# Latent attention: a second set of keys for odd heads, and another order of its pieces

## The chip, the cores and the metric

The kernel runs on one core of a Trainium2 chip. Its time is the device time of one launch in microseconds (us). A core has TensorE (PE; PEld is its weight load), VectorE (DVE), ScalarE (ACT), GpSimd (POOL) and the queue engine SyncE (SP), each of which runs its own instructions in order and waits for the others by semaphores.

## The reference, cut to what matters

One step of a two-layer backbone on 512 latent and 128 prompt tokens. Layer 0 has eight latent-attention (MLA) heads beside eight neighbourhood heads; layer 1 has grouped-query attention; a SwiGLU block follows each. The change lies in the latent heads of layer 0:

```python
def mla_expand(ckv, w_ukv, k_rope):
    kv = (ckv @ w_ukv).reshape(b, L, MLA_HEADS, MLA_NOPE_DIM + MLA_V_DIM)
    k_nope, v = kv[..., :MLA_NOPE_DIM], kv[..., MLA_NOPE_DIM:]
    k_r = jnp.broadcast_to(k_rope[:, :, None, :], (b, L, MLA_HEADS, MLA_ROPE_DIM))
    return jnp.concatenate([k_nope, k_r], axis=-1), v
...
    a_mla = attend_blocked(q, jnp.concatenate([k_lat, k_ctx], axis=1),
                           jnp.concatenate([v_lat, v_ctx], axis=1), MLA_SCALE)
```

The 512 latent queries attend to 640 keys (512 latent and 128 cached), the 128 prompt queries only to the prompt's 128 keys.

## The kernel before, in words

All activations lie with features on partitions. A float32 operand x is split in a rounded high part h and a low part l = x - h, both in the fast matmul type; a product is then three matmuls (h h, h l, l h). So each operand made on the chip costs a copy on ScalarE (h) and a subtraction on VectorE (l).

**Keys.** A key has 64 own features and 64 rows of rotary features (kr, the same for all heads). Two heads share one product `mk` (`k_pieces`, L843): rows 0 to 63 are the even head's own features, rows 64 to 127 the odd head's. There is one tile set for even heads, `kT[.][0]` and one for odd heads, `kT[.][1]` (h and l, 640 columns of which the scores use all), and a small tile `kTp` with the prompt's keys of both. The rotary half of each is written once, in neighbourhood head 6 (L920); the other half is written again for every pair p, by `k_set` (L830) through two products: `k0` (512 latent keys) and `k1` (128 cached and 128 prompt keys).

**Pieces of a head.** Heads run in order 0 to 7. A head h has four score pieces `s0` to `s3` (128 queries by 640 keys: six matmuls `ms`, the negative maximum `mn` on VectorE, the exponential into `mp` on ScalarE, the reciprocal of the sum `mr` on VectorE, the scaling on POOL); then, one head later, `t0` to `t4` (four transposes each into `mt`, split into `mts_0` to `mts_4`) and `v0` to `v4` (matmuls with the values into one bank `mo`). `v3` and `v4` run one head later still, under the names `w3` and `w4`; after them the two halves of `mo` are added into `oM` by way of `mhs`. `sp` is the prompt's scores (`mpp0s` for pair 0), `pt` the transposes of a pair's two prompt weights and their split (`mpp0pth`, `mpp0ptl`), `pv` the product with the prompt's values (`mpp0o`), then added into `oM`. `q0` and `q1` make the next head's query (`mq`; `mqt` on VectorE, `mqh` on ScalarE, `mql` on POOL). `oNs` are splits of the neighbourhood heads' outputs, put in behind the last exponential of heads 0, 2, 4 and 5, and `oaw` weights of the following projection.

**Order.** The order of the pieces on TensorE is written by hand, in `MLA_ORDER` (L999), one string for even and one for odd heads, and in `NA_ORDER` (L880) for the neighbourhood heads, of which the last, head 7, makes the first pair's keys and query. Each piece is issued behind the last matmul of the piece ahead; the order on ScalarE, VectorE and POOL is set by a scheduler out of the dependencies.

In an odd head, `k0` and `k1` write the even set's rows at once. The odd set is still read by this very head's `s3` and `sp`, so its rows are written by separate pieces, `e0` behind `s3` and `e1` behind `sp`; until then the products' PSUM banks stay taken.

**PSUM.** The pool `m` has four banks, used in turn by all of `q`, `t`, `pt`, `pv`, `k`, `sp` and `mo`; `mo` is held from `v0` of a head to `w4` in the next. The scores have two double banks of their own (`bank2`), so `s2` waits until the exponential of `s0` is done.

Of the kernel before, what the change touches and what calls it, by code (L numbers as in the profile page):

```python
# [12 lines left out]
F32R = mybir.dt.float32r  # L13
# [38 lines left out]
def body(ctx, tc, xT, vecs, crow, wm0, wm0g1, wm0g, wm1, wA, wNV, wNA, wMK, wMV, wOA, wGQ, wGK, wGV, wOC,  # L52
# [130 lines left out]
    def mm3(ps, a, b, h, l, st, sp, **k):  # L183
        PE.matmul(ps, a, h, start=st, stop=False, **k)
        PE.matmul(ps, a, l, start=False, stop=False, **k)
        PE.matmul(ps, b, h, start=False, stop=sp, **k)
# [217 lines left out]
    def scores(pss, q, kh, kl):  # L404

        a, b = q
        for i, (c0, c1) in enumerate(HALF):
            PE.matmul(pss[:, i, :HT], a, kh[:, c0:c1], start=True, stop=False)
        for i, (c0, c1) in enumerate(HALF):
            PE.matmul(pss[:, i, :HT], a, kl[:, c0:c1], start=False, stop=False)  # L410
        for i, (c0, c1) in enumerate(HALF):
            PE.matmul(pss[:, i, :HT], b, kh[:, c0:c1], start=False, stop=True)
# [90 lines left out]
    hh, hl = hm.hh, hm.hl  # L503
    pss = [pair(f"wA{u}") for u in range(2)] + [[bank(f"wA2{c}") for c in range(2)]]
# [7 lines left out]
    with tc.tile_pool(name="start", bufs=1) as big:  # L512
# [9 lines left out]
        w3 = [unit(wA[0], 1024, "wA0")]  # L522
# [50 lines left out]
    kr = keep.tile([P, 768], F32, name="kr")  # L573
# [22 lines left out]
    for c, (c0, c1) in enumerate(HALF):  # L596
        ps = pss[2][c]
        V.tensor_tensor(ka[0:32, c0:c1], ps[0:32, :HT], tk[0:32, c0:c1], ALU.mult)
        done = V.tensor_tensor(kb[0:32, c0:c1], ps[32:64, :HT], tk[32:64, c0:c1], ALU.mult)
# [3 lines left out]
    pss = [pair(f"ckv{u}") for u in range(2)]  # L603
# [15 lines left out]
    for kk in range(4):  # L619
# [3 lines left out]
        for j in range(2):  # L623
            k = 2 * kk + j
            a, b = wh[:, 512 * j:512 * (j + 1)], wl[:, 512 * j:512 * (j + 1)]
            for i in range(5):
                c0, c1 = P * i, P * i + P
# [19 lines left out]
    for r in range(2):  # L647
        hr, lr = STACK[r]
        src = ckf[hr, :512].rearrange("p (a b) -> p a b", b=P)
# [177 lines left out]

    KPART = ((0, 512), (512, 640), (640, 768))

    def k_set(r, rows, parts, src):  # L830

        jobs = []
        for c in parts:
            c0, c1 = KPART[c]
            o = c0 - KPART[parts[0]][0]
            h, l = [(kTp[i][r] if c == 2 else kT[i][r][:, c0:c1])[rows] for i in range(2)]
            jobs.append((h, l, src[rows, o:o + c1 - c0]))
        for h, l, part in jobs:
            S.activation(h, part, AF.Copy)
        for h, l, part in jobs:  # L840
            V.tensor_tensor(l, part, f(h), ALU.subtract)

    def k_pieces(p, bk):  # L843

        out = {}
        for c, n in ((0, 512), (1, 256)):
            parts, box = ((0,), (1, 2))[c], []

            def done(ps, parts=parts, box=box):
                box.append(ps)  # L850
                k_set(0, slice(0, 64), parts, ps)

            def other(parts=parts, box=box):
                k_set(1, slice(64, 128), parts, box[0])
            (out[f"k{c}"],) = pieces_of(f"mk{p}{c}", bk, lambda: mla_w(p), *[t for t in lat[c]], [0, 1], 0, n, done)
            out[f"e{c}"] = other
        return out

    mqs, exps = {}, {}
# [14 lines left out]
    def ybank(name):  # L874
# [4 lines left out]
    tail, oN = {}, []  # L879
    NA_ORDER = ["s0 q0 t0 t1 q1 m0 q2 s1 v0 t2 sp q3 q4 v1 q5 m1 v2 q6 pt q7 m2 pv",  # L880
                "s0 q0 t0 t1 q1 m0 q2 s1 v0 t2 sp q3 q4 v1 q5 q6 q7 m1 v2 pt m2 pv"] * 3
    NA_ORDER += ["s0 t0 t1 pt m0 s1 v0 t2 sp m1 v1 pv v2 m2", "s0 t0 t1 k0 s1 e0 v0 t2 sp k1 v1 u0 e1 v2 u1"]
    M_AT = 1, 3, 5, 6
    for h in range(8):
        p, r = divmod(h, 2)
        if r == 0:
            oN.append(ring.tile([P, T], F32, tag="x", name=f"oN{p}"))
            pfirst, psecond = prompt_pair([nv[4][:, 2 * p + i, :] for i in range(2)], oN[p], ab, f"npp{p}",
                                         lambda name: bank(name, "y"))
        pts = []  # L890
        sc = na_scores(h, bm, pts)
        if h < 7:
            bm = na_bias(h + 1)
        qh, ql, ks = [t[r] for t in nqk[p]]
        pieces = named("s", sc)

        def prompt_scores(pss, qh=qh, ql=ql, ks=ks):
            PE.matmul(pss, qh[:, NS:T], ks[:, 896:1024], start=True, stop=False)
            PE.matmul(pss, ql[:, NS:T], ks[:, 896:1024], start=False, stop=True)
        pieces["sp"] = pfirst(r, prompt_scores)  # L900
        if p < 3:
            pieces.update(named("q", na_q(p + 1) if r == 0 else na_k(p + 1)))
        for n, at in enumerate(M_AT):
            if h == at:
                pieces.update(named("n" if "m0" in pieces else "m", mod0(4 + n, lambda n=n: bank(f"mod{4 + n}", "y"), mod_raw)))
        if h == 7:
            pieces.update(k_pieces(0, ybank))
            pieces.update(named("u", q_pieces(0, ybank, lambda c: ring.tile([P, T], F32R, tag="h" + c, name=f"mq{c}0"),
                                              lazy(lambda: load(tabM[:, 0, :], T, "tq0")))))
        sequence(NA_ORDER[h], {**pieces, **tail})  # L910
        tail = na_values(h, pts, oN[p])
        if r == 1:
            tail.update(psecond)
        if h == 6:
            cqs = [rsplit(cq[u], f"cqs{u}") for u in range(2)]
            lat = latents()
            kT = [[ring.tile([P, T], F32R, tag="h" + c, name=f"kT{c}{r}") for r in range(2)] for c in "hl"]
            kTp = ring.tile([P, T], F32R, tag="x", name="kTp")
            kTp = [[kTp[:, P * (2 * i + r):P * (2 * i + r + 1)] for r in range(2)] for i in range(2)]
            for r in range(2):  # L920
                k_set(r, (slice(64, 128), slice(0, 64))[r], (0, 1, 2), kr)
            mla_w(0)
            wmv = unit(wMV, 1024, "wmv")
# [17 lines left out]
    tq = cp.tile([P, 2, T], F32, name="tq")  # L941
    nc.sync.dma_start(tq, tabM)
    mv = [cp.tile([P, 8, P], F32R, name=f"mv{i}") for i in range(6)]
    for i, pss in mvb.items():
        vsplit(mv[i], pss)
    open_y(s=2)
# [4 lines left out]
    def mla_scores(h, pts):  # L951
        r = h % 2
        ll = tiny.tile([P, 4], F32, tag="ll", bufs=4, name=f"ml{h}")

        def piece(j):
            qh, ql = mqs[h]
            pss = bank2(f"ms{h}_{j}")
            scores(pss, (qh[:, P * j:P * j + P], ql[:, P * j:P * j + P]), kT[0][r], kT[1][r])
            nm = tiny.tile([P, 1], F32, tag="nm", name=f"mn{h}_{j}")
            V.tensor_reduce(nm, pss[:, :, :HT], AX.XY, ALU.max, negate=True)  # L960
            pt = cp.tile([P, T], F32, tag="mp", bufs=8, name=f"mp{h}_{j}")
            exps[h, j] = S.activation(halves(pt), pss[:, :, :HT], AF.Exp, bias=nm, accum_out=ll[:, j:j + 1])
            softmax_tail(pt, ll[:, j:j + 1], f"mr{h}_{j}", T)
            pts.append(pt)
        return [lambda j=j: piece(j) for j in range(4)]
# [28 lines left out]
    for i in range(6):  # L994
        if i not in mvb and i not in BESIDE:
            mv_late(i)
    tail, oM, oNs = {}, [], []

    MLA_ORDER = ("s0 w3 q0 w4 s1 t0 t1 pt s2 v0 t2 q1 v1 t3 s3 pv v2 t4 sp",  # L999
                 "s0 w3 q0 w4 s1 t0 t1 q1 s2 k0 v0 t2 s3 e0 v1 k1 t3 sp e1 t4 v2")  # L1000
    late = {}
    for h in range(8):
        p, r = divmod(h, 2)
        if r == 0:
            oM.append(cp.tile([P, T], F32, tag="om", bufs=4, name=f"oM{p}"))
            pfirst, psecond = prompt_pair([mv[5][:, 2 * p + i, :] for i in range(2)], oM[p], cp, f"mpp{p}",
                                         bank)
        pts = []
        sc = mla_scores(h, pts)
        qh, ql = mqs[h]  # L1010
        pieces = named("s", sc)
        pieces["sp"] = pfirst(r, lambda pss, qh=qh, ql=ql, r=r: mm3(pss, qh[:, NS:T], ql[:, NS:T], kTp[0][r], kTp[1][r], True, True))
        if h == 0:
            pieces.update({f"b{i}": lambda i=i: mv_late(i) for i in BESIDE})
        if h < 7:
            pieces.update(named("q", mla_q(h + 1)))
            if r == 1:
                pieces.update(k_pieces(p + 1, qbank))
        sequence(MLA_ORDER[r], {**pieces, **late, **{k: v for k, v in tail.items() if k not in ("v3", "v4")}})
        late = {"w" + k[1]: tail[k] for k in ("v3", "v4") if k in tail}  # L1020

        def out_m(ps, h=h, p=p, r=r):
            half_sum(((oM[p][64 * r:64 * r + 64, 0:NS], 0, NS),), ps, NS, cp, f"mhs{h}")
        tail = values(h, pts, lambda b, th, tl, h=h: [(mv[b][:, h, :], th), (mv[b][:, h, :], tl)], cp, "m", out_m)
        if r == 1:
            tail.update(psecond)
        if h in (0, 2, 4, 5):
            oNs.append(after(exps[h, 3], lambda: rsplit(oN[len(oNs)], f"oNs{len(oNs)}")))
# [654 lines left out]
    hh, hl = box2["m"].hh, box2["m"].hl  # L1683
# [374 lines left out]
```

## Time and profile before

| | us |
|---|---|
| median of 3 runs | 1501.86 (1498.52 to 1502.44) |
| profiled execution | 1503.23 |
| its span, first to last instruction | 1501.2 |
| busy TensorE / VectorE / ScalarE / POOL | 1448.7 / 1233.7 / 786.2 / 176.3 |
| the latent heads, first score matmul to the last head's | 223.76 to 321.17 |

One execution was profiled. "L64" in its rows is line 64 of the kernel, the helper through which all matmuls go; so a matmul is told by its tiles: `ms<-kTh,mqh` writes tile ms from kTh and mqh. A row of a timeline gives the start, the length, the engine, the line, the operation, output and inputs, and in brackets how long the engine stood idle ahead of it and who ended that. The timeline merges like neighbours (x4). "PEclk" is the share of full TensorE clock that was granted.

### The profile page before, as it was taken

To read this page: it belongs to the slowest core of one execution; us is meant where nothing else is said; L and a number is where in the kernel's file an instruction comes from. 1 tells how busy PE (TensorE), PEld (TensorE's weight loads), DVE (VectorE), ACT (ScalarE), POOL (GpSimd) and SP (SyncE) were. 2 spreads that over 40 slices of the span, in tenths; PEclk is the share of its full clock that TensorE was granted. 3 is DMA by queue.
4 is the path that set the end of the run, shared out by engine and by line. 5 is a ranking of instruction groups with operands and counts; after the bars stand their busy time and mean duration, and the time that the engine had idled before them with its cause. 6 is when DMAs were issued, how large, how long until landed. Compare 5 with 4: busy or idle time off the path is not lost. (4 is left out here: it accounts for less than half of the span.)

```text
span 1501.2 us, 25833 instructions
## 1 busy us (share of the span) xinstructions
PE 1448.7 (96%) x9766; PEld 1392.8 (93%) x9766; DVE 1233.7 (82%) x2375; ACT 786.2 (52%) x1539; POOL 176.3 (12%) x272
## 2 busy tenths in 40 slices
PE   5999989899999999999999999999999999999997
PEld 4989978889899999999999999989899999999996
DVE  5877778877788888955898887887899989889976
ACT  5446677763635555532122656673565555655443
POOL 0046636420000000000000122220100000000000
PEclk9999999999999999999999999999999999999999
DMA  9653341015055555549775311115245555548561
GB/s 375 202 152 121 114 145 43 15 64 204 29 207 164 170 171 168 162 169 341 231 229 169 103 33 36 37 41 185 68 157 169 193 170 191 175 154 297 181 263 71
DMA packets 79636, 231.48 MB, mean 154 GB/s; under 512 B 8856, under 2 KB 13240, under 8 KB 79128
## 3 DMA queue, kind: packets, MB, share of 16 engines
q1 hardware_dynamic: 77152, 225.43, 45.0%
q10 hardware_dynamic: 1944, 3.48, 0.7%
q8 instruction: 76, 1.25, 0.3%
q0 software_dynamic: 416, 0.93, 0.2%
q14 instruction: 48, 0.39, 0.1%
HBM read 193.15 MB, written 36.66 MB: 153 GB/s over the span
## 5 line engine op out<-in xcount | busy, mean ns | idle before, releaser
L1627 DVE SCALAR_TENSOR_TENSOR junk<-wm,cb 128x1024 bf16<-128x1024 f32 x88 | 107.2, 1218 | 3.4 <-DMA wm<-in_wm 2.8
L64 PE MATMUL gq<-h10h,wgq 128*128 128x320 f32 x256 | 65.8, 316 | 0.0
L261 POOL TENSOR_SCALAR h10h<-h10t,gs,mods 128x320 fp32r<-128x320 f32 x4 | 3.1, 787 | 437.7 <-DVE h10t L255 435.4
L1367 ACT ACTIVATE wY<-s 128x1024 fp32r<-128x1024 f32 x37 | 39.2, 1060 | 27.7 <-PE fg L64 24.0
L1893 POOL TENSOR_TENSOR xr<-xw,fn1rs 128x320 f32<-128x320 f32 x2 | 1.7, 860 | 416.9 <-ACT fn1rs L229 416.9
L1367 ACT ACTIVATE wZ<-s 128x1024 fp32r<-128x1024 f32 x37 | 39.1, 1057 | 18.6 <-PE fd L64 16.3
L1368 DVE TENSOR_TENSOR wZ<-s,wZ 128x1024 fp32r<-128x1024 f32 x37 | 45.2, 1222 | 2.9 <-ACT wZ L1367 0.2
L1476 DVE TENSOR_TENSOR sg<-up,sg 128x640 f32<-128x640 f32 x37 | 30.4, 822 | 20.8 <-ACT sg L1475 20.3
L64 PEld LDWEIGHTS gq<-h10h,wgq 128*128 128x128 f32 x256 | 44.9, 189 | 0.6
L1368 DVE TENSOR_TENSOR wY<-s,wY 128x1024 fp32r<-128x1024 f32 x37 | 45.1, 1218 | 0.3
L1475 ACT ACTIVATE sg<-fg 128x320 f32<-128x320 f32 x37 | 16.2, 438 | 48.5 <-PE fg L64 48.5
L64 PE MATMUL fg<-h01q,wgu 128*128 128x320 f32 x192 | 40.3, 316 | 0.9 <-ACT h01q L298 0.5
L1497 ACT ACTIVATE p<-fd 128x320 f32<-128x320 f32 x37 | 16.2, 438 | 46.7 <-PE fd L64 46.7
L1830 ACT ACTIVATE gp<-gs,gb,rq 128x640 f32<-128x640 f32 (+1 forms) x40 | 31.8, 795 | 15.3 <-DVE gb L1829 13.6
L64 PE MATMUL gq<-h10l,wgq 128*128 128x320 f32 x128 | 39.5, 308 | 0.0
L64 PE MATMUL fg<-h11q,wX 128*128 128x320 f32 x228 | 36.7, 309 | 0.0
L64 PE MATMUL fu<-h11q,wX 128*128 128x320 f32 x228 | 36.6, 309 | 0.0
L64 PE MATMUL fd<-h11q,wZ 128*128 128x320 f32 x228 | 36.6, 309 | 0.0
L64 PE MATMUL fg<-h11E,wW 128*128 128x320 f32 x228 | 36.5, 309 | 0.0
L64 PE MATMUL fg<-h11N,wZ 128*128 128x320 f32 x228 | 36.5, 309 | 0.0
L64 PE MATMUL fd<-h11D,wY 128*128 128x320 f32 x228 | 36.4, 308 | 0.0
L64 PE MATMUL fg<-h11C,wY 128*128 128x320 f32 x228 | 36.4, 308 | 0.0
(3399 smaller groups left out, 5323.0 us busy)
## 6 DMA issues: line engine op xcount, KB each, us to landing
wm<-in_wm SPq DMA_DIRECT2D x48, 512.0 KB, 4.2
mraw<-in_wm SPq DMA_DIRECT2D x8, 1024.0 KB, 13.1
mraw<-in_wm SPq DMA_DIRECT2D x16, 512.0 KB, 4.1
wmv<-in_wm0g SPq DMA_DIRECT2D x8, 512.0 KB, 3.9
wm<-in_wm0g SPq DMA_DIRECT2D x8, 512.0 KB, 5.3
ruo<-in_wFO SPq DMA_DIRECT2D x8, 512.0 KB, 4.0
rgo<-in_wFO SPq DMA_DIRECT2D x8, 512.0 KB, 6.0
x<-in_xT SPq DMA_DIRECT2D x8, 320.0 KB, 5.2
```

The source lines that it names most:

```text
L64: cls.last = nc.tensor.matmul(*a, **k)
L261: G.tensor_scalar(h[:, c0:c1], t, self.gsl[:, k, 0:1], self.ml[:, self.sh + k, 0:1], ALU.mult, ALU.add)
L1367: S.activation(h, src, AF.Copy)
L1368: V.tensor_tensor(w_, src, f(h), ALU.subtract)
L1475: last = S.activation(sg[:, 0:HT], g[:, :HT], AF.Silu, scale=-1.0)
L1476: V.tensor_tensor(sg, up, sg, ALU.mult)
L1497: S.activation(p5, b5[:, :HT], AF.Copy)
L1627: V.scalar_tensor_tensor(junk, raw, 1.0, cb[:, c, :], ALU.mult, ALU.mult, accum_out=mods[l][:, j0 + i, c:c + 1])
L1830: S.activation(dst, src, AF.Exp, bias=nb, scale=rq[:, j:j + 1], accum_out=ll[:, j:j + 1])
L1893: G.tensor_tensor(x[k][:, c0:c1], root[1][k], nrm.rs[:, c0:c1], ALU.mult)
```

## The change

```diff
+    def k_tiles(r, p):
+        return odd_keys[p % 2] if r else even_keys
+
-    def k_set(r, rows, parts, src):
+    def k_set(r, rows, parts, src, p=0):
...
-            h, l = [(kTp[i][r] if c == 2 else kT[i][r][:, c0:c1])[rows] for i in range(2)]
+            h, l = [(prompt if c == 2 else main_[:, c0:c1])[rows] for main_, prompt in k_tiles(r, p)]
...
-            parts, box = ((0,), (1, 2))[c], []
-
-            def done(ps, parts=parts, box=box):
-                box.append(ps)
-                k_set(0, slice(0, 64), parts, ps)
-
-            def other(parts=parts, box=box):
-                k_set(1, slice(64, 128), parts, box[0])
+            parts = ((0,), (1, 2))[c]
+
+            def done(ps, parts=parts):
+                for r in range(2):
+                    k_set(r, slice(64 * r, 64 * r + 64), parts, ps, p)
...
-            out[f"e{c}"] = other
...
-    NA_ORDER += ["s0 t0 t1 pt m0 s1 v0 t2 sp m1 v1 pv v2 m2", "s0 t0 t1 k0 s1 e0 v0 t2 sp k1 v1 u0 e1 v2 u1"]
+    NA_ORDER += ["s0 t0 t1 pt m0 s1 v0 t2 sp m1 v1 pv v2 m2", "s0 t0 t1 k0 s1 v0 t2 sp k1 v1 u0 v2 u1"]
...
-            kTp = [[kTp[:, P * (2 * i + r):P * (2 * i + r + 1)] for r in range(2)] for i in range(2)]
+            even_keys, first_odd = [[(kT[i][r], kTp[:, P * (2 * i + r):P * (2 * i + r + 1)]) for i in range(2)] for r in range(2)]
+            odd_keys = [first_odd]
...
+    odd_keys.append([(cp.tile([P, T], F32R, name=f"kTo{c}"), cp.tile([P, P], F32R, name=f"kTq{c}")) for c in "hl"])
+    k_set(1, slice(0, 64), (0, 1, 2), kr, 1)
...
-            scores(pss, (qh[:, P * j:P * j + P], ql[:, P * j:P * j + P]), kT[0][r], kT[1][r])
+            kh, kl = [t[0] for t in k_tiles(r, h // 2)]
+            scores(pss, (qh[:, P * j:P * j + P], ql[:, P * j:P * j + P]), kh, kl)
...
-    MLA_ORDER = ("s0 w3 q0 w4 s1 t0 t1 pt s2 v0 t2 q1 v1 t3 s3 pv v2 t4 sp",
-                 "s0 w3 q0 w4 s1 t0 t1 q1 s2 k0 v0 t2 s3 e0 v1 k1 t3 sp e1 t4 v2")
+    MLA_ORDER = ("s0 w3 q0 w4 s1 t0 t1 pt s2 v0 t2 pv q1 v1 t3 s3 v2 t4 sp",
+                 "s0 w3 q0 w4 s1 k0 t0 t1 q1 s2 v0 k1 t2 s3 v1 t3 v2 sp t4")
```

There are now two sets of odd keys, used in turn by the pairs: `kT[.][1]` for pairs 0 and 2, and new tiles `kTo` and `kTq` for pairs 1 and 3, whose rotary rows are filled ahead of the value splits. `k_set` for both sets runs right behind the product, and `e0` and `e1` are gone. In odd heads `k0` moves to behind `s1`, `k1` to ahead of `t2`, and `v2` and `sp` to ahead of `t4`; in even heads `pv` moves from behind `s3` to behind `t2`. No matmul is added or taken away.

On VectorE, in head 5 (keys of pair 3), from the split of `oNs2` to that of `mts_3`, before; `kTl_2551` is the even set, `kTl_2552` the odd set, 64x512 from `k0` and 64x128 from `k1`:

```order
L462 TENSOR_TENSOR oNs2l<-oN_1953,oNs2h 128x640
L841 TENSOR_TENSOR kTl_2551<-mk_3756,kTh_2549 64x512
L383 RECIPROCAL mr_2r<-ml_3659 128x1
L960 TENSOR_REDUCE mn_3_3784<-ms_3_3777 128x1
L391 TENSOR_TENSOR mts_2l<-mt_2_3768,mts_2h 128x512
L841 TENSOR_TENSOR kTl_2552<-mk_3756,kTh_2550 64x512
L383 RECIPROCAL mr_3r<-ml_3659 128x1
L841 TENSOR_TENSOR kTl_2551<-mk_3795,kTh_2549 64x128
L841 TENSOR_TENSOR kTp<-mk_3795,kTp 64x128
L462 TENSOR_TENSOR oNs3l<-oN_2366,oNs3h 128x640
L391 TENSOR_TENSOR mts_3l<-mt_3_3806,mts_3h 128x512
```

And the same place of the changed kernel, up to the same split of `mts_3`:

```order
L391 TENSOR_TENSOR mts_1l<-mt_1_3743,mts_1h 128x512
L844 TENSOR_TENSOR kTol<-mk_3723,kToh 64x512
L866 TENSOR_TENSOR mqt_3759<-mq_3752,tq 128x320
L963 TENSOR_REDUCE mn_2_3770<-ms_2_3763 128x1
L844 TENSOR_TENSOR kTl_2551<-mk_3780,kTh_2549 64x128
L844 TENSOR_TENSOR kTp<-mk_3780,kTp 64x128
L391 TENSOR_TENSOR mts_2l<-mt_2_3795,mts_2h 128x512
L383 RECIPROCAL mr_2r<-ml_3669 128x1
L963 TENSOR_REDUCE mn_3_3811<-ms_3_3804 128x1
L844 TENSOR_TENSOR kTol<-mk_3780,kToh 64x128
L844 TENSOR_TENSOR kTql<-mk_3780,kTqh 64x128
L391 TENSOR_TENSOR mts_3l<-mt_3_3820,mts_3h 128x512
```

The wide splits now stand ahead of `mn_2`, the odd set's narrow ones (`kTol`, `kTql`) ahead of `mts_3`, and `oNs3l` behind it.

On TensorE, in head 4 (even), around the prompt's values `mpp1o` of pair 1, before:

```order
L64 MATMUL ms_3_3610<-kTh_2549,mqh_3305 128x320 x2
L64 MATMUL ms_3_3610<-kTl_2551,mqh_3305 128x320 x2
L64 MATMUL ms_3_3610<-kTh_2549,mql_3306 128x320 x2
L64 MATMUL mpp1o<-mpp1pth,mv_2813 128x128
L64 MATMUL mpp1o<-mpp1ptl,mv_2813 128x128
L64 MATMUL mpp1o<-mpp1pth,mv_2813 128x128
L64 MATMUL mpp1o<-mpp1ptl,mv_2813 128x128
L64 MATMUL mo_3576<-mts_2h,mv_2810 128x512
```

And in the changed kernel:

```order
L68 MATMUL mt_2_3589<-ident,mp_2_3417 128x128
L68 MATMUL mt_2_3589<-ident,mp_3_3458 128x128
L64 MATMUL mpp1o<-mpp1pth,mv_2813 128x128
L64 MATMUL mpp1o<-mpp1ptl,mv_2813 128x128
L64 MATMUL mpp1o<-mpp1pth,mv_2813 128x128
L64 MATMUL mpp1o<-mpp1ptl,mv_2813 128x128
L64 MATMUL mq_3607<-cqs0h,wm_3336 128x320
```

The four matmuls moved from between `s3` and `v2` to between `t2` and `q1`.

On VectorE, the same head 4, around the split `mpp1ptl` that these matmuls read, before:

```order
L391 TENSOR_TENSOR mts_0l<-mt_0_3537,mts_0h 128x512
L391 TENSOR_TENSOR mts_1l<-mt_1_3546,mts_1h 128x512
L383 RECIPROCAL mr_1r<-ml_3488 128x1
L960 TENSOR_REDUCE mn_2_3569<-ms_2_3562 128x1
L391 TENSOR_TENSOR mpp1ptl<-mpp1t,mpp1pth 128x256
L391 TENSOR_TENSOR mts_2l<-mt_2_3579,mts_2h 128x512
```

And in the changed kernel:

```order
L391 TENSOR_TENSOR mts_0l<-mt_0_3547,mts_0h 128x512
L383 RECIPROCAL mr_1r<-ml_3498 128x1
L963 TENSOR_REDUCE mn_2_3579<-ms_2_3572 128x1
L391 TENSOR_TENSOR mts_1l<-mt_1_3556,mts_1h 128x512
L391 TENSOR_TENSOR mpp1ptl<-mpp1t,mpp1pth 128x256
L391 TENSOR_TENSOR mts_2l<-mt_2_3589,mts_2h 128x512
```

The split stands at the same place, behind the same instructions, with `mts_1l` now behind `mn_2`.

More of the change, by code (lines that the diff above doesn't have):

```diff
@@ L1011, in body @@
         pieces = named("s", sc)
-        pieces["sp"] = pfirst(r, lambda pss, qh=qh, ql=ql, r=r: mm3(pss, qh[:, NS:T], ql[:, NS:T], kTp[0][r], kTp[1][r], True, True))
+        pieces["sp"] = pfirst(r, lambda pss, qh=qh, ql=ql, ks=k_tiles(r, p): mm3(pss, qh[:, NS:T], ql[:, NS:T], ks[0][1], ks[1][1], True, True))
         if h == 0:
```

## The prediction

> **What bounds the kernel now.** First the page: busy shares, then the chain that ended last.
>
> ```profile
> PE 1448.7 (96%) x9766; PEld 1392.8 (93%) x9766; DVE 1233.7 (82%) x2375; ACT 786.2 (52%) x1539; POOL 176.3 (12%) x272
> PE 38%; DVE 4%; ACT 2%; issue 1%; POOL 0%; DVEq 0%; ACTq 0%
> ```
>
> TensorE is the bound. The change takes no matmul away, so only idle TensorE time, or time at a lowered TensorE clock, can be won. The change lies in the latent heads, so the next view is busy time by head: each stretch runs from a head's first score matmul to the next head's, heads 1 to 6 (columns: length, busy PE, PEld, DVE, ACT, POOL, granted clock).
>
> ```profile
> 230.83:244.85 14.02, 12.05 (x78) 10.86 (x79) 10.79 (x27) 11.02 (x29) 9.30 (x11) 1.00 0.12 39
> 244.85:256.28 11.43, 11.01 (x77) 10.18 (x75) 9.56 (x18) 8.46 (x18) 5.25 (x6) 1.00 0.01 2
> 256.28:271.21 14.93, 13.63 (x83) 12.22 (x83) 12.76 (x31) 11.89 (x29) 6.88 (x9) 0.95 0.12 35
> 271.21:283.48 12.27, 11.84 (x76) 11.00 (x75) 9.51 (x17) 8.16 (x18) 4.92 (x5) 0.93 0.02 3
> 283.48:299.44 15.96, 13.71 (x84) 12.30 (x83) 13.89 (x32) 12.41 (x30) 6.46 (x9) 0.92 0.11 32
> 299.44:312.41 12.97, 12.95 (x76) 12.01 (x75) 9.34 (x17) 8.33 (x18) 4.36 (x5) 0.83 0.01 2
> 298.00:300.00 2.00, 2.00 (x9) 1.81 (x8) 1.00 (x4) 0.91 (x3) 0.37 (x1) 0.50 0.00 0
> ```
>
> The odd heads 1, 3 and 5, which make the next pair's keys, lose 1.97, 1.30 and 2.25 us of TensorE time; the even heads 0.42, 0.43 and 0.02. After the idle time of heads 3 and 5 the clock falls: to 0.50 in 298 to 300, and 0.83 on average over head 6. The timeline of TensorE names the gaps (in brackets, with who ended them) and shows what the clock costs.
>
> ```profile
> 234.94 0.77 PE L68 MATMUL mt<-ident,mp 128*128 128x128 f32 x5 [0.88 <-POOL mp L384]
> 242.79 0.44 PE L64 MATMUL mpp0s<-kTp,mqh 128*128 128x128 f32 x2 [0.53 <-DVE kTl L841]
> 243.90 0.66 PE L68 MATMUL mt<-ident,mp 128*128 128x128 f32 x4 [0.56 <-DVE mts_3l L391]
> 247.53 0.46 PE L64 MATMUL ms<-kTh,mqh 128*128 128x320 f32 x2
> 267.47 0.63 PE L68 MATMUL mt<-ident,mp 128*128 128x128 f32 x4 [0.43 <-DVE mts_2l L391]
> 269.51 1.05 PE L68 MATMUL mt<-ident,mp 128*128 128x128 f32 x4 [0.86 <-DVE mts_3l L391]
> 274.73 0.45 PE L64 MATMUL ms<-kTh,mqh 128*128 128x320 f32 x2
> 297.67 1.11 PE L68 MATMUL mt<-ident,mp 128*128 128x128 f32 x4 [1.81 <-DVE mts_3l L391]
> 304.08 0.46 PE L64 MATMUL ms<-kTh,mqh 128*128 128x320 f32 x2
> ```
>
> From t4 of an odd head to s1 of the next head the same pieces run each time (t4 v2 s0 w3 q0 w4). At full clock they take 247.53 - 243.90 = 3.63 us; after head 3, 274.73 - 269.51 = 5.22; after head 5, 304.08 - 297.67 = 6.41. The lowered clock thus costs 1.6 and 2.8 us. With the gaps, odd heads lose 2.0, 1.3 + 1.6 = 2.9, and 2.2 + 2.8 = 5.0 us: **9.9 us is all that the key part could win.**
>
> **Why they wait.** VectorE around the largest gap, head 5:
>
> ```profile
> 292.14 0.68 DVE L841 TENSOR_TENSOR kTl<-mk,kTh 64x512 fp32r<-64x512 f32 x1
> 294.56 0.69 DVE L841 TENSOR_TENSOR kTl<-mk,kTh 64x512 fp32r<-64x512 f32 x1
> 295.49 0.28 DVE L841 TENSOR_TENSOR kTl<-mk,kTh 64x128 fp32r<-64x128 f32 x1
> 295.69 0.27 DVE L841 TENSOR_TENSOR kTp<-mk,kTp 64x128 fp32r<-64x128 f32 x1
> 295.89 1.13 DVE L462 TENSOR_TENSOR oNs3l<-oN,oNs3h 128x640 fp32r<-128x640 f32 x1
> 296.94 0.68 DVE L391 TENSOR_TENSOR mts_3l<-mt,mts_3h 128x512 fp32r<-128x512 f32 x1
> ```
>
> t4 waits for a PSUM bank: one of four holds mo, one holds k1's product until e1, so t4 needs the bank of t3, and mts_3l stands on VectorE behind the second wide key split (0.69), two narrow ones and oNs3l (1.13).
>
> **The change, odd heads.** With other tiles to write, the second rows' splits need not wait for s3 and sp. TensorE runs k0 right after s1, VectorE does both wide splits before s2's maximum, and k1 is freed by its own four narrow splits. The rows for a walk through head 5: where s1 and the maximum mn_1 end, k0's length (289.73 to 291.12, 1.4 us), and groups with minimum, median and maximum of one in ns.
>
> ```profile
> 287.10 0.60 PE L68 MATMUL mt<-ident,mp 128*128 128x128 f32 x4
> 289.73 0.39 PE L64 MATMUL mk<-ckh,wm 128*128 128x512 f32 x1
> 291.12 0.40 PE L64 MATMUL mo<-mts_0h,mv 128*128 128x512 f32 x1
> 287.30 0.82 DVE L960 TENSOR_REDUCE mn<-ms 128x1 f32<-128x640 f32 x1
> L960 DVE TENSOR_REDUCE mn<-ms x32: 798/814/826, 225.2 to 321.7; 128x1 f32<-128x640 f32 x32
> L391 DVE TENSOR_TENSOR mts_1l<-mt,mts_1h x8: 673/680/690, 236.5 to 327.3; 128x512 fp32r<-128x512 f32 x8
> L867 DVE TENSOR_TENSOR mqt<-mq,tq x16: 471/477/492, 211.1 to 309.6; 128x320 f32<-128x320 f32 x16
> ```
>
> An instruction on VectorE starts some 0.05 to 0.08 before the printed end of the one ahead, so I count each that much shorter. From mn_1's end at 288.1: oM 0.6 (a wide split's length), oNs2l 0.74 (mn's length), kTl 0.64, mts_0l and mts_1l 1.25, kTol 0.64, mqt 0.40, mn_2 0.73, kTl and kTp 0.40, mts_2l 0.62, mn_3 0.73, kTol and kTql 0.40, mts_3l 0.65: 7.15 to kTql; with about 1.2 of waits for ScalarE between (it delivers oNs2h, kTh and mr_2's exponential late), kTql ends near 296.5 and mts_3l near 297.2. TensorE reaches v0 0.4 too early (mts_0l), k1 0.15 too early, and t4, near 295.9, waits 0.65 for kTql. So 1.2 of waits replace 5.0: **3.8 us won.** Head 3 has no oNs; there ScalarE takes the first key split before s1's exponential and waits for k0, v0 waits 0.35 and t4 0.5: 2.9 - 0.85, **2.0 won.** In head 1, k0 fills the 0.88 before t0 (POOL is done by then), and some 0.6 stays of the rest: **1.4 won.** Together 7.2.
>
> **The change, even heads.** pv moves from behind s3 to right behind t2. It needs mpp's split on VectorE; head 4:
>
> ```profile
> 278.35 0.80 DVE L960 TENSOR_REDUCE mn<-ms 128x1 f32<-128x640 f32 x1
> 279.07 0.41 DVE L391 TENSOR_TENSOR mpp1ptl<-mpp1t,mpp1pth 128x256 fp32r<-128x256 f32 x1
> 278.41 0.40 PE L64 MATMUL mq<-cqs0h,wm 128*128 128x320 f32 x1
> 283.10 0.44 PE L64 MATMUL mpp2s<-kTp,mqh 128*128 128x128 f32 x2 [0.43 <-DVE mts_3l L391]
> 314.76 0.50 PE L64 MATMUL mo<-mts_4h,mv 128*128 128x512 f32 x1 [0.79 <-ACT mts_4h L390]
> 315.90 0.50 PE L64 MATMUL mo<-mts_4l,mv 128*128 128x512 f32 x1 [0.64 <-DVE mts_4l L391]
> ```
>
> The split ends at 279.07 + 0.41 = 279.48, and the same pieces (mn_2, mts_1l, in another order) still stand ahead of it. TensorE now wants it where q1 began, at 278.41: a **new wait of 1.1 us**, behind which q1, v1, t3 and s3 queue. In return pv takes a bank before q1, so sp, three turns later, gets q1's bank and not t3's, and the 0.43 at sp goes. Another 0.1 or 0.2 comes back where the pieces behind find VectorE ahead. I put heads 2 and 4 at +0.5 each. Head 6 is the same at its start; at its end, where w4 now waits 0.79 + 0.64, ScalarE does mts_4h before the last exponential, so I put it at 0. Together +1.0.
>
> **The change, before the heads.** The first fill of the odd set is three ScalarE and three VectorE instructions ahead of the value splits.
>
> ```profile
> L841 DVE TENSOR_TENSOR kTl<-kr,kTh x4: 284/485/690, 188.3 to 190.5; 64x512 fp32r<-64x512 f32 x2, 64x128 fp32r<-64x128 f32 x2
> 223.23 0.69 DVE L456 TENSOR_TENSOR mv<-mv,mv 128x512 fp32r<-128x512 f32 x1 [0.16 <-ACT mv L455]
> 224.59 0.69 DVE L456 TENSOR_TENSOR mv<-mv,mv 128x512 fp32r<-128x512 f32 x1 [0.67 <-ACT mv L455]
> ```
>
> That is 0.69 + 0.28 + 0.28 = 1.25 us on VectorE, and two waits of 0.83 swallow most of it; the rest reaches head 0's first maximum: between 0 and 0.4, I take 0.2. In the last neighbourhood head, splits move by a place on ScalarE and VectorE; no gap there hangs on them, so 0, with 0.4 either way. What follows the heads starts its transfers when tiles of the heads are released, and TensorE is dense there; it should move as a block.
>
> **The sum.** -7.2 + 1.0 + 0.2 = **-6.0 us**. The profiled execution took 1503.23 (span 1501.2): 1497.2. The median shown, 1501.86, lies 1.37 below it, and I keep that distance: **1495.9**.
>
> [...]
>
> **Rivals.**
> 1. *VectorE is the bound of the odd heads* (chance 0.12). It is busy 13.89 of 15.96 us in head 5, nothing is taken off it, and moved splits only delay others; against it, its work is not late in sum, only in order. Then half of the gaps stay and the clock still falls once: 9.9 / 2 - 2.8 / 2 - 1.2 = about 2.3 won: 1499.5. This is also the case in which a second set does not do what it says.
> 2. *The falls of the clock are chance* (0.13). Gaps of 0.79 and 0.64 within 1.2 us in head 7 lowered nothing, 0.43 and 0.86 in head 3 did; so the profiled falls may be missing in the median run. Then gaps alone are won, 7.2 - 4.4 - 1.2 = 1.6: 1500.3.
> 3. *Slower* (0.09): the new 1.1 us at pv, with 0.3 at v0 just ahead, is as long as head 3's pair of gaps, and lowers the clock in heads 2, 4 and 6, and one odd head keeps its fall as now. Each fall costs up to 2.8; four cost 11.2 against -6.0: 1507.1. It decides from the third fall on.
> 4. *More* (0.06): pv's wait is absorbed and odd heads keep no wait: 9.9 + 1.4 = 11 won, 1491.
>
> **Chances.** The forecast has 0.60, for 4.5 to 9 won. About 0.3% (4.5 us) is what a measurement of this kernel can tell from no change. Faster by more: forecast and rival 4, less a little at the edge, 0.63. Rivals 1 and 2 and that edge: same, 0.30. Slower, 0.07: rival 3, less the part with only three falls. The range goes from rival 4, 1490.5, past rivals 1 and 2, to 1502.5, which leaves out rival 3.
>
> **What would show it.** Right: no gap above 0.7 us before t4 of heads 1, 3 and 5; clock 1.00 in all heads; a gap near 1 us ahead of the mpp product in heads 2 and 4; head 5 with its following w4 3 to 4 us shorter. Wrong: a clock below 0.9 in even heads, t4 still waiting on mts_3l, or a loss behind the heads.

## The result

The changed kernel takes **1498.09 us** (median of 14 runs, 1495.15 to 1499.47) against 1501.68 (14 runs, 1498.52 to 1506.9) of the kernel before on the same chip: ratio **0.9973, 95% interval [0.9965, 0.9982]**. It is faster by 3.6 us, a quarter of a per cent, surely more than nothing, but less than the 6.0 us that the prediction summed. Its profiled execution took 1497.4 us (span 1495.3), which is 5.8 below the profiled one of before; the profiles differ by more than the medians, and the reason is the main finding below.

### The profile page after: what moved, and what is told of

It reads as the page before. It is cut to its first block, busy times and chain, and to the rows that moved or that the text cites. A ratio compares the mean times of both kernels' runs of the same rounds, so it can differ in the third digit from the quotient of the medians.

```text
span 1495.3 us, 25840 instructions
## 1 busy us (share of the span) xinstructions
PE 1448.1 (97%) x9766; PEld 1391.3 (93%) x9766; DVE 1235.8 (83%) x2378; ACT 786.6 (53%) x1542; POOL 178.0 (12%) x272
```

## The profile after

The page of the changed kernel, busy shares and chain:

```profile
PE 1448.1 (97%) x9766; PEld 1391.3 (93%) x9766; DVE 1235.8 (83%) x2378; ACT 786.6 (53%) x1542; POOL 178.0 (12%) x272
PE 38%; DVE 4%; ACT 2%; issue 1%; POOL 0%; DVEq 0%; ACTq 0%
```

TensorE is still the bound (97% busy), and the first fill shows as three instructions more on VectorE and on ScalarE. Busy time by head, heads 1 to 6 (columns as in the prediction):

```profile
231.35:243.97 12.62, 11.88 (x77) 10.67 (x78) 10.23 (x24) 10.12 (x26) 8.51 (x10) 1.00 0.13 43
243.97:256.00 12.03, 11.38 (x79) 10.32 (x77) 10.08 (x22) 8.73 (x20) 5.71 (x7) 1.00 0.00 1
256.00:269.14 13.14, 12.65 (x84) 11.41 (x83) 12.17 (x27) 11.34 (x27) 6.08 (x8) 1.00 0.12 41
269.14:281.20 12.06, 11.37 (x78) 10.32 (x77) 9.98 (x22) 8.73 (x20) 5.71 (x7) 1.00 0.00 1
281.20:294.85 13.65, 12.76 (x84) 11.38 (x83) 12.32 (x27) 11.32 (x28) 5.56 (x8) 1.00 0.10 39
294.85:306.88 12.03, 11.45 (x79) 10.28 (x77) 11.53 (x24) 10.11 (x23) 5.45 (x7) 1.00 0.01 2
```

The odd heads now lose 0.74, 0.49 and 0.89 us of TensorE time in place of 1.97, 1.30 and 2.25. The even heads lose 0.65, 0.69 and 0.58, more than before (0.42, 0.43, 0.02). The clock is 1.00 in all six. TensorE's timeline names what is left (t4 of heads 1, 3, 5, then pv of heads 2 and 4):

```profile
243.56 0.66 PE L68 MATMUL mt<-ident,mp 128*128 128x128 f32 x4 [0.69 <-DVE kTql L844]
268.72 0.66 PE L68 MATMUL mt<-ident,mp 128*128 128x128 f32 x4 [0.46 <-DVE kTp L844]
294.44 0.66 PE L68 MATMUL mt<-ident,mp 128*128 128x128 f32 x4 [0.69 <-DVE kTql L844]
251.47 0.30 PE L64 MATMUL mpp0o<-mpp0pth,mv 128*128 128x128 f32 x1 [0.65 <-DVE mts_1l L391]
276.68 0.30 PE L64 MATMUL mpp1o<-mpp1pth,mv 128*128 128x128 f32 x1 [0.69 <-ACT mts_2h L390]
```

The last of these rows names ScalarE's mts_2h, but that ends only at 276.69; VectorE's mts_1l ends at 276.53, so it is the same wait as in the row above it. VectorE around t4 of head 5, where the prediction walked:

```profile
289.77 0.69 DVE L844 TENSOR_TENSOR kTol<-mk,kToh 64x512 fp32r<-64x512 f32 x1
290.90 0.81 DVE L963 TENSOR_REDUCE mn<-ms 128x1 f32<-128x640 f32 x1
294.09 0.29 DVE L844 TENSOR_TENSOR kTql<-mk,kTqh 64x128 fp32r<-64x128 f32 x1
294.41 0.69 DVE L391 TENSOR_TENSOR mts_3l<-mt,mts_3h 128x512 fp32r<-128x512 f32 x1
295.43 1.31 DVE L462 TENSOR_TENSOR oNs3l<-oN,oNs3h 128x640 fp32r<-128x640 f32 x1
```

t4 starts with the end of kTql (294.38), not of mts_3l, and oNs3l is behind both. From this head's s1 (283.93) to the end of kTql are 10.45 us; the walk had 296.5 - 286.21 = 10.3.

**Where the time went, by head.** I take the stretch from one head's s1 to the next one's, in a second execution of the kernel before ("before, again", in whose heads the clock falls only once, in head 5, for 1.5 us) and in the profile after:

| stretch from s1 of | before, again | after | difference | predicted |
|---|---|---|---|---|
| head 1 | 14.85 | 13.52 | -1.33 | -1.4 |
| head 2 | 11.46 | 11.99 | +0.53 | +0.5 |
| head 3 | 14.15 | 13.18 | -0.97 | -2.0, with 1.6 of clock |
| head 4 | 11.47 | 12.02 | +0.55 | +0.5 |
| head 5 | 16.63, 15.10 without the clock | 13.80 | -1.30 at full clock | -3.8, with 2.8 of clock |
| head 6 | 12.17 | 12.43 | +0.26 | 0 |

Head 5's v0 waits only 0.21 us (for mts_0l) and head 3's not at all, where the prediction had 0.4 and 0.35. Head 6 keeps one long wait, w4's for the split of t4 (in the changed kernel):

```profile
309.82 0.50 PE L64 MATMUL mo<-mts_4l,mv 128*128 128x512 f32 x1 [1.16 <-DVE mts_4l L391]
```

At full clock the heads, from head 0's first score matmul to head 7's s1, take 88.1 us before (89.67 - 1.53) and 85.9 after: **2.3 us from the gaps themselves.** That measure, "the heads", is used in all that follows; in three profiles of the changed kernel it is 85.87, 85.89 and 85.83, so differences of a few tenths can be read. Behind the heads nothing changes: from head 7's s1 to the end are 1185.7 us in before, again, and 1185.1 after.

## The experiments

The theory after the result: the gaps went as walked, but what a gap costs in clock depends on where it falls in time, so the 4.4 us of clock that the prediction credited are not there in every execution. The rivals: every gap of that size (1.81 us ahead of t4 of head 5, 0.43 and 0.86 in head 3) lowers the clock, theory B in the first two experiments (then 6 us should show in the medians too); and, for the parts, that the order alone, the second set alone, or the even heads' move alone makes the difference. Each kernel was timed beside the kernel before on the same chip; ratios are to that.

**1. The kernel before, again.**

> The kernel before, against itself. [...] Theory B (a gap of this size always lowers the clock): both falls are there again and cost 1.6 and 2.8 us within 0.5. [...]

Measured: 1501.68 us (11 runs), ratio 0.9999 [0.9988, 1.0011]. The stretches of its profile that lie around the same largest gap and around a gap much later in the program:

```profile
293.08:296.49 3.41, 1.20 (x8) 0.83 (x7) 3.32 (x8) 2.50 (x8) 0.80 (x1) 1.00 0.00 0
296.49:299.91 3.42, 3.37 (x13) 3.18 (x14) 1.55 (x5) 1.05 (x3) 0.37 (x1) 0.50 0.00 0
299.91:303.32 3.41, 3.41 (x24) 3.24 (x24) 2.21 (x5) 1.88 (x5) 1.06 (x2) 1.00 0.02 5
869.93:873.35 3.42, 3.42 (x14) 3.42 (x14) 1.37 (x4) 1.84 (x5) 0.00 (x0) 0.50 0.01 2
```

The same program, with the same gap of 1.81 us ahead of t4 of head 5, has the clock at 0.50 for 3.4 us here and had it for 6.8 us in the first profile; the fall of head 3 (0.43 and 0.86 us of gap) is missing, and theory B with it. The first profile cut at the same width:

```profile
266.19:269.60 3.41, 2.11 (x15) 1.56 (x14) 3.31 (x8) 2.62 (x8) 1.24 (x2) 1.00 0.00 0
269.60:273.02 3.42, 3.42 (x13) 3.22 (x14) 1.41 (x5) 1.05 (x3) 0.37 (x1) 0.50 0.00 0
293.50:296.91 3.41, 1.92 (x14) 1.37 (x12) 3.32 (x7) 3.03 (x9) 1.15 (x2) 1.00 0.00 0
296.91:300.32 3.41, 2.65 (x10) 2.46 (x11) 2.26 (x7) 1.06 (x3) 0.37 (x1) 0.50 0.00 0
300.32:303.74 3.42, 3.42 (x13) 3.23 (x12) 0.83 (x2) 0.88 (x2) 0.00 (x0) 0.50 0.02 5
303.74:307.15 3.41, 3.41 (x25) 3.27 (x25) 2.73 (x6) 2.45 (x5) 1.66 (x2) 1.00 0.00 0
```

In the first profile the clock changes at 269.62, 273.04, 296.93 and 303.76 (the rows are cut within 0.03 us of that): the first fall lasts 3.41 us, the second, two steps of that, 6.83, and their starts are 27.31 us apart, 8 steps. In before, again, the two falls start at 296.47 and 869.90: these 573.43 us are 168 steps of 3.413 us. So the measured edges lie on a grid of 3.413 us, fixed through an execution, and at another offset in each: from the first profile to this one the grid is shifted by -0.46, the program by +0.44 at head 0 and by -1.1 at t4 of head 5.

**2. The changed kernel, again.**

> The changed kernel again. [...] Theory B: the falls at 22 and 866 us come again.

Measured: 1499.04 us (12 runs), ratio 0.9978 [0.9967, 0.9988]. Heads 85.9 us, no lowered clock in them; t4's and pv's waits are the same. The fall at 866 us did not come again; one near 21 us did.

**3. The change without its part in even heads** (the key part alone).

```diff
-    MLA_ORDER = ("s0 w3 q0 w4 s1 t0 t1 pt s2 v0 t2 pv q1 v1 t3 s3 v2 t4 sp",
+    MLA_ORDER = ("s0 w3 q0 w4 s1 t0 t1 pt s2 v0 t2 q1 v1 t3 s3 pv v2 t4 sp",
```

> The changed kernel with the even heads' order of before (pv behind s3). Main theory (key part wins, pv move loses): about 1.2 us faster than the changed kernel, so 1496.9 or 0.9965 of before; the gaps of 0.65 and 0.69 ahead of pv go, and the one of about 0.4 at sp of heads 2 and 4 is back. Rival (the even order is needed for the odd gain, since it frees a bank in time): 1500 or 0.999.

Measured: 1499.26 us (12 runs), ratio 0.9985 [0.9976, 0.9995]: a miss, for it should have been faster than the whole change. By the heads it is slower (below); the times, 1499.26 and 1499.04 of the changed kernel on the same chip, do not tell the two apart. Three rows of TensorE (v0 of head 3, q1 of head 4, sp of head 6), and VectorE ahead of the third:

```profile
265.62 0.50 PE L64 MATMUL mo<-mts_0h,mv 128*128 128x512 f32 x1 [0.58 <-DVE mts_0l L391]
278.81 0.38 PE L64 MATMUL mq<-cqs0h,wm 128*128 128x320 f32 x1 [0.70 <-DVE mts_1l L391]
310.91 0.41 PE L64 MATMUL mpp3s<-kTp,mqh 128*128 128x128 f32 x2 [2.16 <-DVE mr_3r L383]
```

```profile
308.25 1.91 DVE L174 TENSOR_TENSOR oaw<-oaw2r,oaw 128x1024 fp32r<-128x1024 f32 x1
310.08 0.68 DVE L391 TENSOR_TENSOR mts_3l<-mt,mts_3h 128x512 fp32r<-128x512 f32 x1
```

Three things are to be seen. The wait of 0.7 us that the prediction put down to pv is there without pv's move: q1 takes its place and waits for t1's bank, since VectorE now does mts_1l behind the maximum of s2, and that order comes with the key part. And without pv's move, sp of head 6 needs the bank of t3, whose split stands behind the 1.91 us of oaw: a gap of 2.16 that neither other kernel has, and with a fall of the clock behind it in this profile. (The row names the reciprocal mr_3r, which ends at 310.84; mts_3l, just ahead of it, ends at 310.76.) Third, v0 of heads 3 and 5 waits 0.58 us for mts_0l, where the whole change has 0 and 0.21; why mts_0l comes later there is not traced. Heads 88.4, less 0.9 of lowered clock, 87.5 us. That is 1.6 above the whole change, of which 0.87 lies in head 3, 0.36 in head 5 and only 0.39 in head 6: the gap of 2.16 stands there in place of the 0.26 at pv and the 1.16 at w4 that the changed kernel has.

**4. The kernel before with the changed order of even heads** (pv's move alone).

```diff
-    MLA_ORDER = ("s0 w3 q0 w4 s1 t0 t1 pt s2 v0 t2 q1 v1 t3 s3 pv v2 t4 sp",
+    MLA_ORDER = ("s0 w3 q0 w4 s1 t0 t1 pt s2 v0 t2 pv q1 v1 t3 s3 v2 t4 sp",
```

> The kernel before with the even heads' order of the change (pv behind t2) alone. Main theory: a wait of 0.6 to 1.1 us at pv of heads 2, 4 and 6 is new, 0.4 at sp goes, so 0.5 to 2 us slower: 1502.9 or 1.0008. Rival (pv sooner is the useful part): 2 us or more faster, 0.9987 or less.

Measured: 1503.25 us (12 runs), ratio 1.0008 [0.9998, 1.0019], as expected, though the interval takes in no change at all. Heads 88.7: three waits of 0.72 us for the split that pv reads, against 0.43 at sp that went. Its t4 of head 5 waits just as before, and the clock stays up. TensorE's timeline at t4 and at the s1 behind it, then the stretch with the gap and the one behind it:

```profile
297.91 0.66 PE L68 MATMUL mt<-ident,mp 128*128 128x128 f32 x4 [1.81 <-DVE mts_3l L391]
301.55 0.46 PE L64 MATMUL ms<-kTh,mqh 128*128 128x320 f32 x2
```

```profile
296.07:299.49 3.42, 1.61 (x12) 1.50 (x12) 2.84 (x8) 1.95 (x6) 0.89 (x2) 1.00 0.00 0
299.49:302.90 3.41, 3.41 (x24) 3.23 (x24) 2.40 (x5) 1.84 (x4) 0.79 (x2) 1.00 0.02 5
```

From t4 to s1 are 3.64 us, which is the 3.63 of full clock. So a gap of 1.81 us lowered the clock for 6.8 us, for 3.4 us and not at all, in three executions whose work there is the same. It begins 2.35, 1.68 and 0.00 us behind an edge of the grid in them.

**5. The second set with the old places** (odd rows split right behind their product, k0, k1, sp and v2 where they were).

```diff
-                 "s0 w3 q0 w4 s1 k0 t0 t1 q1 s2 v0 k1 t2 s3 v1 t3 v2 sp t4")
+                 "s0 w3 q0 w4 s1 t0 t1 q1 s2 k0 v0 t2 s3 v1 k1 t3 sp t4 v2")
```

and the even heads' order of before.

> The kernel before with the second set of odd keys and the odd rows split right behind their product, but with k0, k1, sp and v2 at their old places in odd heads, and the even heads' order of before. Main theory (the win needs the key products ahead of s2 and t2, so that VectorE has their splits out of the way before the split of t3): the odd rows' wide split now stands behind the first one, still late, and t4 of heads 3 and 5 still waits, up to 1 us; the heads, from head 0's first score matmul to the second of head 7, take about 87.5 us at full clock (88.1 before, 85.9 after), time about 1501.2, ratio 0.9995. Rival (the second set alone, which frees the products' banks at once, is what wins): no gap over 0.7 us at t4, heads 86.4, ratio 0.9985 like the kernel with the key part alone, or lower.

Measured: 1501.76 us (12 runs), ratio 1.0003 [0.999, 1.0017]; heads 87.9 us. The set alone wins nothing that the time shows, and 0.2 us in the heads; t4 still waits, 0.80 us in head 3 and, longer than the 1 us expected, in head 5:

```profile
297.52 0.66 PE L68 MATMUL mt<-ident,mp 128*128 128x128 f32 x4 [1.62 <-DVE mts_3l L391]
```

**6. The odd heads' new order with one set** (e0 kept behind s3, e1 behind sp).

```diff
-                 "s0 w3 q0 w4 s1 t0 t1 q1 s2 k0 v0 t2 s3 e0 v1 k1 t3 sp e1 t4 v2")
+                 "s0 w3 q0 w4 s1 k0 t0 t1 q1 s2 v0 k1 t2 s3 e0 v1 t3 v2 sp e1 t4")
```

> The kernel before with the changed order of the odd heads but one set of odd keys: e0 still behind s3, e1 still behind sp. Main theory (the order can only be had with the second set): k0's product now holds its bank from behind s1 to behind s3, k1's from ahead of t2 to behind sp, with mo a third one, so that one bank is left for t2, t3 and sp; TensorE waits in every odd head for the splits, 2 to 5 us each in heads 1, 3 and 5, heads 93 to 100 us, time 1507 to 1515, ratio 1.004 to 1.008. Rival (the order is what wins and the second set brings nothing): ratio 0.9985 to 0.999.

Measured: 1506.13 us (12 runs), ratio 1.0035 [1.0021, 1.0048]; heads 92.6 us at full clock (94.0 as they stand; from t4 to s1 the fall behind head 5 costs 4.58 - 3.18 = 1.4, beside the same pieces behind head 3). Slower, a little less so than expected. Head 5's t3 and t4:

```profile
297.94 0.63 PE L68 MATMUL mt<-ident,mp 128*128 128x128 f32 x4 [1.19 <-DVE mts_2l L391]
301.05 1.11 PE L68 MATMUL mt<-ident,mp 128*128 128x128 f32 x4 [1.75 <-DVE mts_3l L391]
```

With k0's and k1's products held until e0 and e1, each transpose waits for the split of the one ahead. So neither half of the key part wins alone: the order needs the second set, and the set is worth nothing without the order.

**7. pv one place later** in the changed kernel.

```diff
-    MLA_ORDER = ("s0 w3 q0 w4 s1 t0 t1 pt s2 v0 t2 pv q1 v1 t3 s3 v2 t4 sp",
+    MLA_ORDER = ("s0 w3 q0 w4 s1 t0 t1 pt s2 v0 t2 q1 pv v1 t3 s3 v2 t4 sp",
```

> The changed kernel with pv one place later in even heads (t2 q1 pv v1). The key part alone left a wait of 2.16 us at sp of head 6 that neither other kernel has. Theory (a question of banks: sp takes t3's bank there, whose split mts_3l stands behind the 1.2 to 1.9 us split of oaw on VectorE; pv ahead of t3 turns the banks by one, so sp gets another): here sp gets pv's own bank, freed by the two adds into oM, which stand behind oaw but ahead of mts_3l, so sp of head 6 waits 0.8 to 1.6 us; and q1 waits 0.6 for mts_1l in heads 2 and 4, as with the key part alone. Heads 86.5 to 87.2 us at full clock (85.9 in the changed kernel, 87.5 with the key part alone), ratio to the kernel before 0.9982. Rival (pv's early place in time, not its bank, is what takes the 2.16 away, because VectorE then runs the adds early): sp still waits 2 us or more, heads 87.5, ratio 0.9985 to 0.999.

Measured: 1500.39 us (12 runs), ratio 0.9988 [0.9978, 0.9998]; heads 86.9 us. On VectorE oaw stands ahead of both adds into oM and of mts_3l, and yet sp of head 6 waits little (VectorE behind oaw, then sp):

```profile
307.81 0.58 DVE L448 TENSOR_TENSOR oM<-mpp2o,mpp2h 64x128 f32<-64x128 f32 x2
308.44 0.69 DVE L391 TENSOR_TENSOR mts_3l<-mt,mts_3h 128x512 fp32r<-128x512 f32 x1
308.54 0.41 PE L64 MATMUL mpp3s<-kTp,mqh 128*128 128x128 f32 x2 [0.49 <-ACT mts_3h L390]
```

Here `sp` starts behind the adds, which end at 308.39 (and behind mts_3h, which the row names, at 308.41), and ahead of the end of mts_3l at 309.13. With the key part alone it started behind mts_3l (310.76) and ahead of the end of the adds (311.32). So it is a matter of which bank sp gets. The bank is not all of the difference between 2.16 and 0.49: had sp waited for mts_3l here too, the gap would have been about 1.2 (an estimate: 0.15 behind 309.13), since oaw takes 1.22 us here against 1.91. That the heads lie in the range of the theory is luck: v0 of heads 3 and 5 waits 1.00 and 0.99, which it did not have, and w4 of head 6 does not wait. The ratio, whose interval takes in both expectations, does not decide.

**8. t4 ahead of sp** in odd heads of the changed kernel, measured twice.

```diff
-                 "s0 w3 q0 w4 s1 k0 t0 t1 q1 s2 v0 k1 t2 s3 v1 t3 v2 sp t4")
+                 "s0 w3 q0 w4 s1 k0 t0 t1 q1 s2 v0 k1 t2 s3 v1 t3 v2 t4 sp")
```

> The changed kernel with t4 ahead of sp in odd heads. Theory (t4's wait of 0.46 to 0.69 us for the odd set's narrow splits in heads 1, 3 and 5 is a wait for k1's bank, which falls to whichever piece takes it): t4 takes another bank and starts at once, sp waits about 0.25 us instead; and mts_1l goes back ahead of the maximum of s2 in heads 2 and 4, which takes off part of their 0.65 us. Heads 84.0 to 84.9 us at full clock (85.9 in the changed kernel), time 1497.2, ratio to the kernel before 0.9968. Rival (VectorE is the bound there, so the wait only moves): the same waits at sp, heads 85.9, ratio 0.9978.

> The changed kernel with t4 ahead of sp, the second time, beside the changed kernel on the same chip. If the 1.1 us that the heads win at full clock count, its time is about 1.1 us below the changed kernel's, ratio to the kernel before 0.997; if what the heads win is lost in the noise of the clock, the two agree within 0.4 us.

Measured: 1496.86 us (12 runs), ratio 0.9972 [0.996, 0.9985], and 1496.95 (5 runs), 0.9966 [0.9954, 0.9978], beside 1497.30 of the changed kernel on the same chip; heads 84.8 us both times. By the heads it is the better kernel, 1.1 us below the changed one; the medians beside each other differ by 0.35 us, so what the heads win is not resolved there. sp of head 5:

```profile
294.71 0.44 PE L64 MATMUL mpp2s<-kTp,mqh 128*128 128x128 f32 x2 [0.53 <-DVE kTql L844]
```

The wait in odd heads only moved from t4 to sp (0.53 in place of 0.69), as the rival said: odd heads win 0.3 us in all. The even heads win the other 0.8 (0.17, 0.18 and 0.44 in heads 2, 4 and 6).

**9. s3 ahead of pv** in even heads of the changed kernel.

```diff
-    MLA_ORDER = ("s0 w3 q0 w4 s1 t0 t1 pt s2 v0 t2 pv q1 v1 t3 s3 v2 t4 sp",
+    MLA_ORDER = ("s0 w3 q0 w4 s1 t0 t1 pt s2 v0 t2 s3 pv q1 v1 t3 v2 t4 sp",
```

> The changed kernel with s3 moved ahead of pv in even heads (t2 s3 pv q1 v1 t3 v2 t4 sp). Theory (the 0.65 us ahead of pv in heads 2 and 4 is a wait for VectorE's split of t1, and six score matmuls of 1.2 us cover it): no gap there, heads 84.6 us at full clock, time 1497.5, ratio 0.997. Rival (s3's double bank, or the maximum of s3 put ahead of the splits on VectorE, makes TensorE wait as long): heads 85.9 or more, ratio 0.9978 or above.

Measured: 1498.55 us (12 runs), ratio 0.9984 [0.9971, 0.9997]; heads 86.3 us: the rival. The wait at pv is gone and stands a few pieces later, for the split of t3 behind oaw:

```profile
280.14 1.33 DVE L174 TENSOR_TENSOR oaw<-oaw1r,oaw 128x1024 fp32r<-128x1024 f32 x1 [0.71 <-ACT oaw L173]
282.12 0.50 PE L64 MATMUL mo<-mts_3l,mv 128*128 128x512 f32 x1 [0.62 <-DVE mts_3l L391]
```

**10. t4 ahead of sp and pv behind q1.**

> The changed kernel with t4 ahead of sp in odd heads and pv behind q1 in even heads. Theory: with t4 first, mts_1l is done early in heads 2 and 4, so q1 finds its bank free, and by the end of q1 (0.95 us) the split mpp1ptl is there too: the 0.72 us ahead of pv in heads 2 and 4 goes; in head 6 sp now gets pv's bank and waits for the adds behind oaw, 0.8 to 1.6 us. Heads 84.0 to 85.0 us at full clock (84.8 with t4 first alone), ratio 0.9965 to 0.9975. Rival (the wait moves to q1 as it did with the key part alone): heads 85.5 or more, ratio 0.9978.

Measured: 1497.61 us (5 runs), ratio 0.9968 [0.9955, 0.9981]; heads 84.2 us, no wait at pv of heads 2 and 4 any more, and 0.78 at q1 of head 6 in place of the expected wait at sp. The shortest heads of all; in the time it can't be told from the kernel of 8, and either beats the kernel before by some 4 to 5 us.

**11. The changed kernel, a third time.**

> The changed kernel again. If the falls of the clock are a matter of phase: heads 85.9 us plus what falls there in this execution, mean granted clock of its runs 0.996 to 0.9965 against 0.9948 to 0.9955 of the kernel before (1.5 to 2 us of the difference in time), ratio 0.9973 to 0.9978. If the changed kernel's heads never see a low clock: none there in this profile either.

Measured: 1497.30 us (5 runs), ratio 0.9968 [0.9956, 0.998]; heads 85.8 us, with no lowered clock in them. The granted clock of its runs is 0.9958 on average, against 0.9942 of the kernel before on that chip; both lie just below what was expected. Its profile has a lowered clock ahead of the heads, where two earlier profiles of this kernel have none (this profile, then the first of the changed kernel, at the same place):

```profile
200.00:202.00 2.00, 2.00 (x12) 2.00 (x11) 1.79 (x6) 1.62 (x5) 1.09 (x2) 0.50 0.71 253
```

```profile
200.00:202.00 2.00, 2.00 (x17) 1.96 (x17) 1.90 (x8) 1.92 (x7) 1.22 (x2) 1.00 0.66 246
```

**What the clock is worth on average.** Four profiles have the old odd heads' gaps: in their heads the lowered clock cost 4.4 us (the first), 1.5 (before, again), 0 (4) and 0 (5): mean 1.5. All three of the changed kernel have none there, nor have the five of experiments 7 to 10; of the nine with the second set and the new odd order, only that with the gap of 2.16 (3) has one. The mean granted clock of every run says the same with more weight: 0.9949 over the 98 runs of the kernel before that have it on record, 0.9961 over 31 of the changed one. Among those 98 runs, 0.001 of clock goes with 0.87 (+-0.08) us; 0.0012 is then 1.05 us. Of the 3.85 us between the mean times (1501.78 and 1497.93) the clock accounts for about 1.0 to 1.5, the gaps for 2.3, and the rest, 0 to 0.5, is within the scatter of these means (standard error 0.36).

## Why the prediction was right or wrong

- **Sign and range held; the size was too large.** 1498.09 lies inside 1490.5 to 1502.5 and 2.2 above 1495.9. At 0.27% it falls just inside what the prediction called "within 0.3%", to which it had given 0.30.
- **The step that failed is the 4.4 us of lowered clock**, 1.6 behind head 3 and 2.8 behind head 5, entered in full into "9.9 us is all that the key part could win". It is a property of the one profiled execution: by experiments 1, 4 and 5 the same gaps, or nearly the same (5), cost 1.5, 0 and 0, and over many runs about 1.0 to 1.5. With 1.0 to 1.5 in its place, the sum is -2.6 to -3.1, and -3.6 was measured.
- **The distance of 1.37 us to the median, which I kept, did no harm**: -6.0 was in effect taken from the median. What the distance was is open; the granted clock of that execution over its whole span, 0.995, is no lower than the mean of 0.9949. Rival 2 was right that the profiled falls need not come again, but too strict: by experiments 1, 4 and 5 they cost 1.5, 0 and 0 us, a matter of phase, and are not all absent. Its 1500.3 is 2.2 above the time.
- **The gap terms were right in sign, and in size but for head 3**: head 1 -1.33 (-1.4), heads 2 and 4 +0.53 and +0.55 (+0.5 each), and without the clock heads 3 and 5 -0.97 and -1.30 (-0.4 and -1.0). t4 waits 0.69, 0.46 and 0.69 us; I had 0.6, 0.5 and 0.65. Head 3 won more than twice what I gave it, for the most part because v0's wait of 0.35 is not there.
- **The even heads' +0.5 was right in size and half right in cause.** I charged it to pv waiting for its split. In head 2 of the changed kernel pv first waits for t1's bank, whose split mts_1l the new order puts behind a maximum (it ends at 251.33, and pv starts at 251.47); but pv's own split ends only at 251.65, and its second matmul starts at 251.71. Either wait alone gives as much: 0.65 and 0.70 at q1 with pv left where it was (3), and 0.72 for the split itself where mts_1l comes early (4 and 8):

```profile
277.19 0.33 PE L64 MATMUL mpp1o<-mpp1ptl,mv 128*128 128x128 f32 x1 [0.72 <-DVE mpp1ptl L391]
```

- **The two parts do not add, and I added them.** In the heads the key part alone wins 0.6 us and pv's move alone loses 0.6; together they win 2.3. I gave pv's other effect 0.43 at sp. With the key part in place it is worth 1.6: 1.2 from v0 of heads 3 and 5, and 0.4 in head 6, where it keeps sp off t3's bank (3).
- **The signs named there**: no gap above 0.7 us at t4, clock 1.00 in all heads, and head 5 with what follows 4.1 us shorter than in the first profile (17.87 to 13.80) came true. The last is luck, since 2.8 of it is the first profile's lowered clock; against before, again, it is 2.8 in all (16.63 to 13.80). The gap at pv is 0.65 to 0.69, not near 1.
- **Head 6** lost 0.26 where I had 0. The first fill (+0.2) can't be seen: head 0 starts at 223.5 to 225.5 in the profiles of all kernels.
- **Rivals 1, 3 and 4** fell: VectorE kept no wide split in the way, no clock falls in the even heads of the changed kernel, and waits did remain.

## What to carry to other kernels

Before a lowered clock in one profile is entered into a sum, see in a second execution whether the same gap lowers it again; its cost is a mean over executions (4.4, 1.5, 0 and 0 us here), not what one profile shows. Sum the gaps apart from the clock, and compare them by a stretch at full clock: here the heads repeat within 0.06 us (85.83 to 85.89 in three profiles), the times of the same kernel only within 4.3 (1495.15 to 1499.47). Where pieces take banks in turn, moving one piece changes the bank, and so the releaser, of every piece behind it: two edits that each win little or lose can win together, and a piece's wait must be read from the split that frees its bank. Here the second buffer pays only with the order that it makes possible, and that order only with the buffer.

## What the runs showed of the hardware

In these profiles the granted clock changes only on a grid of 3.413 us, which runs through the execution and starts elsewhere in each: the falls of the changed kernel's first profile start at 22.87 and 865.96 us, 247 steps apart, and those of before, again, 168 (experiment 1). In all fourteen profiles, every lowered stretch between 20 and 1480 us is one or two grid steps long (3.41 or 6.83 us). How busy TensorE is in the step ahead does not decide alone: 2.53 us busy of 3.41 were followed by a lowered step in the grid step from 866.52 of before, again, and 1.61 were not, in that from 296.07 of experiment 4.

Where a gap lies in its step did matter for one gap. All kernels here have the same gap of 0.88 us between 861 and 873 us, in layer 1. It lowered the clock in seven of the fourteen profiles: in all seven in which it begins 0.31 to 0.59 us behind an edge of the grid, and in none of the seven in which it begins 0.70 to 2.97 us behind one. In before, again, it begins at 866.80, and the edge lies at 866.49 (lowered); with the key part alone at 869.22, and the edge at 868.52 (not lowered):

```profile
867.68 0.56 PE L64 MATMUL gs<-gkh,gqh 128*128 128x320 f32 x2 [0.88 <-ACT gqh L1794]
870.10 0.55 PE L64 MATMUL gs<-gkh,gqh 128*128 128x320 f32 x2 [0.88 <-ACT gqh L1797]
```

What it is in the step that decides stays open.
